# Score, similarity and meta-token matmuls contract 128 partitions, with zero halves per head

## The chip, the core and the metric

The kernel runs on one core of a Trainium2 chip. The metric is the device time of one execution in microseconds (us), the median of several runs. TensorE (PE in the profile) multiplies matrices into PSUM, ScalarE (ACT) and VectorE (DVE) do the work on elements, GpSimd (POOL) is almost unused, and SyncE (SP) issues the loads.

## The reference

A trunk of two layers over 272 tokens (16 learned meta tokens and 256 of the sequence), width 1024. The change touches the two token mixers of a layer:

```python
# retention, per head (64 wide q and k, 128 wide v), both directions, in chunks
s   = einsum(q, k) * decay_in
o   = einsum(s, v) + einsum(q * decay, state)
# attention, 8 query heads on 2 key heads, 64 wide, window of 128 and the meta tokens for all
s_band = where(valid, einsum(qb, kband) * scale, -1e30)
s_meta = einsum(qb, meta_k) * scale
p = softmax(concat([s_sink, s_meta, s_band]))
o = einsum(p_meta, meta_v) + einsum(p_band, vband)
...
```

Both read projections of the normed input (`u @ w_in`) and feed `w_ret_o` and `w_att_o`; then come gates, `w_mix_o`, and a squared-ReLU MLP.

## The kernel before

The whole state lies in SBUF with channels on partitions and the 272 tokens (`T`) along the free dimension. Weights come from HBM in units of 128 x 1024, one after another in the order of use; `unit` rounds each to a high part (`wh`, ACT, L128) and a remainder (`wl`, DVE, L129), in rings of four. Every product is three matmuls of such parts, high x high, high x low, low x high (`mm3`, L133 to L135), so precision is kept at the fast matmul type (fp32r). `product` and `proj` run 8 x 3 of them for one output block of 128 channels.

Attention and retention need single heads, which are 64 wide, so two heads lie on one tile of 128 partitions. The high x high and one mixed product of a head are taken in one matmul of 128 rows, by laying the high part on one half of the partitions and the low part on the other (`ka[0]`, `ka[1]`, `qa`, `qk`). The remaining mixed product is a matmul over the 64 partitions of that head alone: L520 in `score` (with `ka[2]`) and L615 in `similar` (with `ql`).

The 16 meta tokens are handled as groups of 32 columns (2 heads x 16): three groups in 96 columns or partitions (`thrice`, `kblk`, `vblk`, `vm`, `vmp`, `pmk`, `ptm`, `tm`), high, low and high again. `meta` (L585) multiplies the meta keys in `kblk` by the queries in three matmuls (L594).

The order of the work is written out by hand and then fixed by a scheduling layer at build time. `value_r`, `key_a` and `query_a` project the values and attention's keys and queries. Then eight heads of attention run: `score(hh + 1)`, `turned(hh)` (transposes of the softmax), `attended` for each pair of heads; eight heads of retention follow: `similar(hh + 1)`, `retained(hh)`, `normed(hh)`. Between these, `fill(n)` puts matmuls of the remaining projections from `queue` on PE, so that PE has work while ACT and DVE finish a softmax. For layer 0 the meta queries have a softmax of their own (L490 to L506, tiles in `m0`).

Tiles are taken from pools of one, two or four buffers by tag: a new tile of a tag waits until the oldest one of that tag is read for the last time. The tags here are `ex` (the exponentials of softmax), `pn` (the normed probabilities), `ptm`, and for retention `tt` and `tb` (the decay) and `sd` (the decayed similarities).

## Time and profile before

| | |
|---|---|
| median of 3 runs | 910.5 us (909.09 to 910.96) |
| span of the profiled execution, first to last instruction | 907.6 us |
| median less that span (work around the span, and spread) | 2.9 us |
| busy: PE, DVE, ACT, POOL | 893.5, 622.1, 561.0, 0.2 us |
| the chain that ended last, by engine | PE 92%, DVE 4% |

Busy time is the time in which at least one instruction of an engine runs. Matmuls overlap in PE's pipeline, so a row that lasts 0.29 us can be followed by the next one after 0.13 us; what a matmul costs is the distance from its start to the next one's. The profile's own time is that of one execution; the runs are timed by themselves.

### The profile page before, as it was taken

What the parts mean: (1) busy time and instruction counts of PE and PEld (TensorE: products, weight loads), DVE (VectorE), ACT (ScalarE), POOL (GpSimd) and SP (SyncE); (2) the same over time, 40 slices, a digit from 0 to 9 for tenths busy, and PEclk for the clock granted to TensorE, in tenths of its full rate; (3) what the DMA queues carried; (4) which work ended last, traced back from release to release, by engine and by line L of the source; (5) the groups of instructions that cost most, each with busy time, mean ns of one, the idle gap of its engine ahead of it and who ended that gap; (6) DMA issues with size and microseconds to landing.
All of it is one profiled execution on the core that took longest, in us unless ns stands there. A gap on an engine that the chain in (4) does not pass through costs nothing.

```text
span 907.6 us, 16590 instructions
## 1 busy us (share of the span) xinstructions
PE 893.5 (98%) x6506; PEld 846.6 (93%) x6506; DVE 622.1 (69%) x1215; ACT 561.0 (62%) x1038; POOL 0.2 (0%) x4
## 2 busy tenths in 40 slices
PE   9999999999999999999999999999999999999997
PEld 8999998999999999999989989989999999998885
DVE  7898888777668655444459898887777765554443
ACT  6757767666467777543455577776665588783432
POOL 0000000000000000000000000000000000000000
PEclk9999999999999999999999999999999999999999
DMA  7653433345554656555544544433456466666661
GB/s 249 197 158 94 140 117 97 113 147 163 181 163 126 200 165 181 168 183 168 181 118 146 157 121 136 139 117 117 128 160 188 129 198 201 188 205 185 183 189 70
DMA packets 41838, 142.15 MB, mean 157 GB/s; under 512 B 5408, under 2 KB 7584, under 8 KB 41760
## 3 DMA queue, kind: packets, MB, share of 16 engines
q1 hardware_dynamic: 41616, 140.96, 51.2%
q8 instruction: 51, 0.84, 0.4%
q14 instruction: 27, 0.22, 0.1%
q10 hardware_dynamic: 144, 0.13, 0.0%
HBM read 140.02 MB, written 1.05 MB: 155 GB/s over the span
## 4 chain that ended last, share of the span: by engine, by line
PE 92%; DVE 4%; ACT 1%; DMA 1%; SPq 1%; issue 1%; DVEq 0%; ACTq 0%
PE ps_a L133 15%; PE ps_a L134 14%; PE ps_a L135 14%; PE ps_s L135 5%; PE ps_s L134 5%; PE ps_s L133 5%; PE ps_t L133 4%; PE ps_t L134 4%; PE ps_t L135 4%; PE ps_s L781 2%; PE ps_a L781 2%; PE ps_a L780 2%; PE ps_s L780 2%; PE ps_a L782 2%; PE ps_s L782 2%; PE ps_o L554 2%
## 5 line engine op out<-in xcount | busy, mean ns | idle before, releaser
L129 DVE TENSOR_TENSOR wl<-raw,wh 128x1024 fp32r<-128x1024 f32 (+2 forms) x264 | 318.2, 1207 | 209.0 <-ACT wh L128 207.1
L128 ACT ACTIVATE wh<-raw 128x1024 fp32r<-128x1024 f32 (+2 forms) x261 | 272.4, 1045 | 218.9 <-PE ps_a L134 74.3
L133 PE MATMUL ps_a<-uh,wh 128*128 128x272 f32 (+1 forms) x920 | 271.0, 295 | 3.8 <-ACT uh L230 3.1
L135 PE MATMUL ps_a<-uh,wl 128*128 128x272 f32 (+1 forms) x920 | 263.3, 286 | 0.0
L134 PE MATMUL ps_a<-ul,wh 128*128 128x272 f32 (+1 forms) x920 | 263.1, 286 | 0.2
L133 PEld LDWEIGHTS ps_a<-uh,wh 128*128 128x128 f32 x920 | 173.4, 188 | 7.7 <-ACT uh L230 3.7
L134 PEld LDWEIGHTS ps_a<-ul,wh 128*128 128x128 f32 x920 | 173.3, 188 | 2.2 <-DVE ul L88 0.8
L135 PEld LDWEIGHTS ps_a<-uh,wl 128*128 128x128 f32 x920 | 173.2, 188 | 0.6 <-DVE wl L129 0.3
L135 PE MATMUL ps_s<-uh,wl 128*128 128x272 f32 (+1 forms) x184 | 53.4, 290 | 0.3 <-DVE wl L129 0.3
L134 PE MATMUL ps_s<-ul,wh 128*128 128x272 f32 (+1 forms) x184 | 53.1, 288 | 0.0
L133 PE MATMUL ps_s<-uh,wh 128*128 128x272 f32 (+1 forms) x184 | 53.0, 289 | 0.0
L133 PE MATMUL ps_t<-uh,wh 128*128 128x272 f32 (+1 forms) x144 | 41.3, 287 | 1.3 <-ACT uh L230 1.3
L134 PE MATMUL ps_t<-ul,wh 128*128 128x272 f32 (+1 forms) x144 | 41.2, 286 | 0.0
L135 PE MATMUL ps_t<-uh,wl 128*128 128x272 f32 (+1 forms) x144 | 41.1, 285 | 0.0
L135 PEld LDWEIGHTS ps_s<-uh,wl 128*128 128x128 f32 x184 | 35.3, 192 | 0.7 <-DVE wl L129 0.7
L133 PEld LDWEIGHTS ps_s<-uh,wh 128*128 128x128 f32 x184 | 35.4, 192 | 0.0
L134 PEld LDWEIGHTS ps_s<-ul,wh 128*128 128x128 f32 x184 | 35.3, 192 | 0.0
L133 PEld LDWEIGHTS ps_t<-uh,wh 128*128 128x128 f32 x144 | 27.2, 189 | 1.5 <-ACT uh L230 1.5
L92 DVE TENSOR_TENSOR fl<-ft,fh 128x272 fp32r<-128x272 f32 (+1 forms) x64 | 27.6, 433 | 0.9 <-ACT fh L91 0.9
L91 ACT ACTIVATE fh<-ft 128x272 fp32r<-128x272 f32 (+1 forms) x64 | 27.1, 424 | 1.7
L709 ACT ACTIVATE ft<-ft 128x272 f32<-128x272 f32 (+1 forms) x64 | 27.1, 424 | 1.6
L133 PE MATMUL ps_a<-fh,wh 128*128 128x272 f32 x96 | 27.8, 290 | 0.0
(296 smaller groups left out, 1937.8 us busy)
## 6 DMA issues: line engine op xcount, KB each, us to landing
raw<-in_w SPq DMA_DIRECT2D x258, 512.0 KB, 3.6
h<-in_h_in SPq DMA_DIRECT2D x8, 136.0 KB, 2.9
tab<-in_tabs SPq DMA_DIRECT2D x2, 544.0 KB, 5.4
out<-yt SPq DMA_DIRECT2D x3, 256.0 KB, 2.0
raw<-in_w SPq DMA_DIRECT2D x4, 128.0 KB, 3.3
raw<-in_w SPq DMA_DIRECT2D x2, 256.0 KB, 4.5
gj<-in_grow SPq DMA_DIRECT2D x1, 512.0 KB, 4.7
mats<-in_mats SPq DMA_DIRECT2D x1, 320.0 KB, 5.2
```

The lines of the kernel that those rows point to most:

```text
L91: A.activation(xh, x, AF.Copy)
L92: V.tensor_tensor(out=xl, in0=x, in1=f(xh), op=sub)
L128: rounded.append(A.activation(wh[:, c], raw[:, c], AF.Copy).ins)
L129: V.tensor_tensor(out=wl[:, c], in0=raw[:, c], in1=f(wh[:, c]), op=sub)
L133: PE.matmul(ps, ah, bh, start=first, stop=False)
L134: PE.matmul(ps, ah, bl, start=False, stop=False)
L135: return PE.matmul(ps, al, bh, start=False, stop=last)
L554: PE.matmul(po[:, c0:], va_pad[c][:, 64 * gg:64 * gg + P], pts[2 * t + gg][:, c, c0:], start=gg == 0 and c == 0, stop=False)
L709: A.activation(t2[:, c0:], t1[:, c0:], AF.Square)
L780: PE.matmul(pss[i], xh, wh[:, sl], start=kk == 0, stop=False)
L781: PE.matmul(pss[i], xh, wl[:, sl], start=False, stop=False)
L782: PE.matmul(pss[i], xl, wh[:, sl], start=False, stop=kk == KF - 1)
```

## The change

The low parts get tiles of their own, of 128 partitions with zeros in the half of the other head: `kal` for attention's keys, and `ql1` beside `ql` for the odd heads of retention. L520, L615 and the third matmul of `meta` then contract 128 partitions. The meta groups become four of 32 (128 columns or partitions); the fourth is low x low, and `meta` runs a fourth matmul. The remainder groups of `vm` and `vmp` are now two ranges of partitions (`odds`), each with an instruction of its own. The constants that must be zero are cleared by GpSimd. To make room, `ex` uses the buffers of `tt`, `ptm` those of `tb`, and `pn` those of `sd`.

```diff
     def zeros(shape, name, dt=F32):
         t = const.tile(shape, dt, name=name)
-        V.memset(f(t) if dt == F32R else t, 0.0)
+        nc.gpsimd.memset(f(t) if dt == F32R else t, 0.0)
         return t
 
-    kblk = [zeros([P, 4, 3, 32], f"kblk{i}", F32R) for i in range(3)]
-    vblk = zeros([P, 3, 32], "vblk")
-    lows, highs = slice(32, 64), slice(64, 96)
-
-    def thrice(x):
-        return x.unsqueeze(1).to_broadcast([x.shape[0], 3, 16])
+    kblk = [zeros([P, 4, 4, 32], f"kblk{i}", F32R) for i in range(3)]
+    vblk = zeros([P, 4, 32], "vblk")
+    kal = zeros([P, 2, T], "kal", F32R)
+    ql1 = zeros([P, 4, T], "ql1", F32R)
+    lows, odds = slice(64, 128), (slice(32, 64), slice(96, 128))
+
+    def fourfold(x):
+        return x.unsqueeze(1).to_broadcast([x.shape[0], 4, 16])
...
-                    low = vm[highs, 4 * q:4 * q + 4]
-                    V.tensor_tensor(out=low, in0=tpm[highs], in1=f(low), op=sub)
+                    for r in odds:
+                        low = vm[r, 4 * q:4 * q + 4]
+                        V.tensor_tensor(out=low, in0=tpm[r], in1=f(low), op=sub)
...
-            for a in halves:
-                V.tensor_tensor(out=ka[2][a], in0=r[a], in1=f(ka[a is halves[1]][a]), op=sub)
+            for a in range(2):
+                V.tensor_tensor(out=kal[halves[a], a], in0=r[halves[a]], in1=f(ka[a][halves[a]]), op=sub)
...
-        V.tensor_copy(vmp, tp[:96, 256:384])
-        V.tensor_tensor(out=vmp[highs], in0=tp[highs, 256:384], in1=f(vmp[highs]), op=sub)
+        V.tensor_copy(vmp, tp[:, 256:384])
+        for r in odds:
+            V.tensor_tensor(out=vmp[r], in0=tp[r, 256:384], in1=f(vmp[r]), op=sub)
...
+        ql = slot("10b", "ql", (4, T), F32R), ql1
+        nc.gpsimd.memset(f(ql[0][halves[1]]), 0.0)
...
-                        V.tensor_tensor(out=ql[hi, i, cc:], in0=r[hi, cc:], in1=f(x), op=sub)
+                        V.tensor_tensor(out=ql[a][hi, i, cc:], in0=r[hi, cc:], in1=f(x), op=sub)
...
-            ex = two.tile([P, T + 1], F32, tag="ex", name="ex")
+            ex = two.tile([P, T + 1], F32, tag="tt", name="ex")
...
-            for c in range(3):
+            for c in range(4):
...
                 PE.matmul(ps[:, :T], qa[:, gg, t, sl], ka[gg], start=True, stop=False)
-                PE.matmul(ps[:, :T], qa[r, gg, t, sl], ka[2][r], start=False, stop=True)
+                PE.matmul(ps[:, :T], qa[:, gg, t, sl], kal[:, gg], start=False, stop=True)
...
-                pn = two.tile([P, SEQ], F32, tag="pn", name="pn", bufs=4)
+                pn = four.tile([P, SEQ], F32, tag="sd", name="pn")
...
-                ptm = two.tile([96, T], F32R, tag="ptm", name="ptm")
+                ptm = two.tile([P, T], F32R, tag="tb", name="ptm")
...
-            ps = bank("s", [T])[:96]
-            for i, q in enumerate((qk[0][:, 0, t], qk[0][:, 1, t], ql[:, t])):
-                PE.matmul(ps[:, c0:], kblk[i][:, t], q[:, c0:], start=i == 0, stop=i == 2)
...
+            ps = bank("s", [T])
+            for i, q in enumerate((qk[0][:, 0, t], qk[0][:, 1, t], ql[0][:, t], ql[1][:, t])):
+                PE.matmul(ps[:, c0:], kblk[min(i, 2)][:, t], q[:, c0:], start=i == 0, stop=i == 3)
...
                 PE.matmul(ps[:, c0:T], qk[1][:, gg, t, sl], qk[0][:, gg, t, c0:], start=True, stop=False)
-                PE.matmul(ps[:, c0:T], qk[1][r, gg, t, sl], ql[r, t, c0:], start=False, stop=True)
+                PE.matmul(ps[:, c0:T], qk[1][:, gg, t, sl], ql[gg][:, t, c0:], start=False, stop=True)
```

Line numbers of the kernel after are two to four higher in this part of the program. PE's order around the first two steps of retention in layer 0, before (L594 is the meta product, L614 and L615 are a similarity step, L133 to L135 fill):

```order
824 L594 MATMUL ps_s<-qk,kblk_113 96x272
825 L594 MATMUL ps_s<-qk,kblk_115 96x272
826 L594 MATMUL ps_s<-ql,kblk_117 96x272
...
833 L614 MATMUL ps_s<-qk,qkl 128x272
834 L615 MATMUL ps_s<-ql,qkl 128x272
835 L614 MATMUL ps_s<-qk,qkl 128x272
836 L615 MATMUL ps_s<-ql,qkl 128x272
```

The same place on PE after the change (L598, L617 and L618 are those lines now; ql_123 is the tile `ql1`):

```order
824 L598 MATMUL ps_s<-qk,kblk_113 128x272
825 L598 MATMUL ps_s<-qk,kblk_115 128x272
826 L598 MATMUL ps_s<-ql,kblk_117 128x272
827 L598 MATMUL ps_s<-ql_123,kblk_117 128x272
...
834 L617 MATMUL ps_s<-qk,qkl 128x272
835 L618 MATMUL ps_s<-ql_123,qkl 128x272
836 L617 MATMUL ps_s<-qk,qkl 128x272
837 L618 MATMUL ps_s<-ql_123,qkl 128x272
```

The meta product has a fourth matmul, the similarity step for an odd head reads `ql1`, and nothing else has moved here. DVE's order in the value projections of layer 0, where `vm` is written (wl is the rounding of weights, tt the decay for retention), before:

```order
44 L129 TENSOR_TENSOR wl<-raw,wh 128x1024
45 L372 TENSOR_TENSOR vm<-ps_s,vm 32x512
46 L361 COPY pads<-vt 128x3x16
47 L129 TENSOR_TENSOR wl<-raw,wh 128x1024
48 L88 SCALAR_TENSOR_TENSOR tab<-tab,rb 128x272 x2
49 L327 TENSOR_TENSOR t_443<-ps_a,tab 128x272
50 L129 TENSOR_TENSOR wl<-raw,wh 128x1024
51 L328 STREAM_SHUFFLE t_444<-t_443 128x272
52 L608 TENSOR_TENSOR tt<-tt,tb 128x128
```

The same place on DVE after the change:

```order
41 L129 TENSOR_TENSOR wl<-raw,wh 128x1024
42 L375 TENSOR_TENSOR vm<-ps_s,vm 32x512 x2
43 L129 TENSOR_TENSOR wl<-raw,wh 128x1024
44 L329 TENSOR_TENSOR t_447<-ps_a,tab 128x272
45 L88 SCALAR_TENSOR_TENSOR tab<-tab,rb 128x272
46 L330 STREAM_SHUFFLE t_448<-t_447 128x272
47 L129 TENSOR_TENSOR wl<-raw,wh 128x1024
```

The instruction on `vm` is doubled, and the product of `tt` and `tb` has left. ACT's order at the end of attention in layer 0 shows where the decay of retention is built after the change (`pn` belongs to the last score, L609 to L611 are the exponentials for `tt` and `tb`, L594 here is the `tb` of `meta`):

```order
119 L529 ACTIVATE pn<-ex,rs 128x256 x2
120 L609 ACTIVATE tt<-rel,de 128x256
121 L610 ACTIVATE tt<-rel,de 128x144
122 L128 ACTIVATE wh<-raw 128x1024
...
130 L550 ACTIVATE ptm<-ps_t 128x272
131 L611 ACTIVATE tb<-rel,de 128x128
132 L128 ACTIVATE wh<-raw 128x1024
133 L594 ACTIVATE tb<-relm,dem 128x16
```

Before, the first two of these sets stood in the value projections, ahead of attention; now they stand behind the last softmax.

## Rows read from the trace of the kernel before

**Rows 1.** The page: span, and busy time of the engines

```profile
span 907.6 us, 16590 instructions
...
PE 893.5 (98%) x6506; PEld 846.6 (93%) x6506; DVE 622.1 (69%) x1215; ACT 561.0 (62%) x1038; POOL 0.2 (0%) x4
```

**Rows 2.** Waits of PE: total us, times, longest

```profile
PE ps_s L364 <- DVE pads L361: 0.6, 1, 0.6
```

**Rows 3.** PE in time, first similarity step, layer 0: start, duration, instruction, operands

```profile
134.44 0.29 PE L135 MATMUL ps_a<-uh,wl 128*128 128x272 f32 x1
134.57 0.28 PE L614 MATMUL ps_s<-qk,qkl 128*128 128x272 f32 x1
134.78 0.39 PE L615 MATMUL ps_s<-ql,qkl 64*128 64x272 f32 x1
135.10 0.39 PE L614 MATMUL ps_s<-qk,qkl 128*128 128x272 f32 x1
135.42 0.39 PE L615 MATMUL ps_s<-ql,qkl 64*128 64x272 f32 x1
135.74 0.39 PE L133 MATMUL ps_a<-uh,wh 128*128 128x272 f32 x1
135.97 0.29 PE L134 MATMUL ps_a<-ul,wh 128*128 128x272 f32 x1
```

**Rows 4.** PE in time, a later step of retention, layer 0

```profile
151.51 0.42 PE L594 MATMUL ps_s<-qk,kblk 128*96 128x272 f32 x2
151.77 0.29 PE L594 MATMUL ps_s<-ql,kblk 128*96 128x272 f32 x1
151.89 0.29 PE L133 MATMUL ps_a<-uh,wh 128*128 128x272 f32 x1
...
152.90 0.49 PE L133 MATMUL ps_a<-uh,wh 128*128 128x272 f32 x1
153.22 0.29 PE L134 MATMUL ps_a<-ul,wh 128*128 128x272 f32 x1
...
157.72 0.49 PE L626 MATMUL ps_o<-tm,vm 96*128 96x272 f32 x1
158.05 0.29 PE L133 MATMUL ps_a<-uh,wh 128*128 128x272 f32 x1
```

**Rows 5.** Lines L520, L615: count, min/median/max ns, first and last start

```profile
L520 PE MATMUL ps_s<-ka,qa x32: 385/388/393, 62.1 to 576.0; 64*128 64x272 f32 x32
L615 PE MATMUL ps_s<-ql,qkl x32: 378/384/391, 134.8 to 643.5; 64*128 64x272 f32 x16, 64*128 64x256 f32 x16
```

**Rows 6.** Windows: stretch, length, busy per engine (instructions), clock, DMA

```profile
45.00:62.00 17.00, 16.47 (x127) 16.13 (x127) 16.22 (x40) 8.90 (x14) 0.00 (x0) 1.00 0.56 169
91.99:109.05 17.06, 17.06 (x122) 15.63 (x120) 14.34 (x42) 11.47 (x28) 0.00 (x0) 1.00 0.44 125
549.87:566.07 16.20, 16.20 (x119) 14.90 (x118) 14.14 (x43) 12.22 (x30) 0.00 (x0) 1.00 0.39 128
604.00:642.00 38.00, 38.00 (x268) 34.78 (x268) 28.95 (x63) 22.43 (x50) 0.00 (x0) 1.00 0.40 119
```

**Rows 7.** Lines L372 and L608 on DVE: count, min/median/max ns

```profile
L372 DVE TENSOR_TENSOR vm<-ps_s,vm x4: 689/689/689, 31.1 to 514.5; 32x512 fp32r<-32x512 f32 x4
L608 DVE TENSOR_TENSOR tt<-tt,tb x16: 274/284/294, 35.8 to 630.7; 128x128 f32<-128x128 f32 x16
```

**Rows 8.** DVE, ACT, PE in time: first softmaxes of layers 0 and 1

```profile
63.13 0.35 DVE L398 TENSOR_SCALAR m<-t 64x16 f32<-64x16 f32 x2
...
63.53 0.72 PE L492 MATMUL ps_s<-m 128*128 128x272 f32 x2
...
526.17 0.49 ACT L525 ACTIVATE pn<-ex,rs 128x256 f32<-128x256 f32 x1
...
527.04 0.44 PE L532 MATMUL ps_t<-mats,pn 128*128 128x128 f32 x2
```

**Rows 9.** Line L272 on DVE: clearing constants

```profile
L272 DVE MEMSET kblk<- x3: 378/378/378, 1.0 to 1.8; 128x384 f32 x3
L272 DVE MEMSET vblk<- x1: 138/138/138, 2.2 to 2.2; 128x96 f32 x1
```

More of the change, by code (lines that the diff above doesn't have):

```diff
@@ L331, in rotated @@
             return t2
-        pads = slot("10a", "pads", (4, 192))
-        vtm = pads[:, 0:2].rearrange("p a (b c k) -> p (a b) c k", b=2, c=3)
-        va_pad = [pads[:, 2], pads[:, 3]]
+        pads = slot("10a", "pads", (896,))
+        vtm = pads[:, 0:512].rearrange("p (a c k) -> p a c k", a=4, c=4)
+        va_pad = [pads[:, 512:704], pads[:, 704:896]]
         V.memset(pads, 0.0)
         vr = slot(2, "vr", (2, D))
-        vm = one.tile([96, 8, P], F32R, tag="vm", name="vm")
+        vm = one.tile([P, 8, P], F32R, tag="vm", name="vm")
         if l == 0:
@@ L342, in encoder @@
             m0 = slot(7, "m0", (2176,))
-            qblk, pm, pmblk, pmt, ka0 = (m0[:, a:b] for a, b in ((0, 512), (512, 784), (784, 1168), (1168, 1424), (1424, 1696)))
+            qblk, pm, pmblk, pmt, ka0 = (m0[:, a:b] for a, b in ((0, 512), (512, 784), (784, 1296), (1296, 1552), (1552, 1824)))
             V.memset(qblk, 0.0)
         es_sb, mask, rel_sb, relm_sb, skn, skmn, de, dem = cst
-        ka = [one.tile([P, T], F32R, tag=f"ka{i}", name="ka") for i in range(3)]
+        ka = [one.tile([P, T], F32R, tag=f"ka{i}", name="ka") for i in range(2)]
         halves = slice(0, 64), slice(64, 128)
@@ L355, in value_r @@
             if m == 0:
-                tpv[q] = bank("s", [4, P])[:96], [bank("t") for _ in range(2)]
+                tpv[q] = bank("s", [4, P]), [bank("t") for _ in range(2)]
             tpm, tps = tpv[q]
@@ L360, in value_r @@
             mine = vtm[:, m]
-            V.tensor_copy(mine[:, :, 16 * (m % 2):16 * (m % 2) + 16], thrice(vt[:, 0:16]))
+            V.tensor_copy(mine[:, :, 16 * (m % 2):16 * (m % 2) + 16], fourfold(vt[:, 0:16]))
             def centre():
@@ L411, in encoder @@
             stt(tab[:, i], tab[:, i], -0.5, rb)
-        vmp = one.tile([96, P], F32R, tag="vmp", name="vmp")
+        vmp = one.tile([P, P], F32R, tag="vmp", name="vmp")
         for gg in range(2):
-            V.tensor_copy(vblk[64 * gg:64 * gg + 64, :, 16 * gg:16 * gg + 16], thrice(vat[64 * gg:64 * gg + 64, 0:16]))
+            V.tensor_copy(vblk[64 * gg:64 * gg + 64, :, 16 * gg:16 * gg + 16], fourfold(vat[64 * gg:64 * gg + 64, 0:16]))
         tp = bank("t")
@@ L495, in encoder @@
             V.tensor_scalar(out=pm, in0=ex[:, :T], scalar1=rs, scalar2=None, op0=mul)
-            for c in range(3):
+            for c in range(4):
                 V.tensor_tensor(
-                    out=pmblk.rearrange("p (t c g k) -> p t c g k", t=4, c=3, g=2)[:, :, c],
+                    out=pmblk.rearrange("p (t c g k) -> p t c g k", t=4, c=4, g=2)[:, :, c],
                     in0=mat["blk"].rearrange("p (t g k) -> p t g k", t=4, g=2),
@@ L511, in score @@
             t, gg = hh // 2, hh % 2
-            r = slice(64 * gg, 64 * gg + 64)
             if gg == 0:
-                pmk[t] = two.tile([P, 2, 3, 32], F32, tag="pmk", name="pmk")
+                pmk[t] = two.tile([P, 2, 4, 32], F32, tag="pmk", name="pmk")
             pns[hh] = []
@@ L519, in score @@
                 PE.matmul(ps[:, :T], qa[:, gg, t, sl], ka[gg], start=True, stop=False)
-                PE.matmul(ps[:, :T], qa[r, gg, t, sl], ka[2][r], start=False, stop=True)
+                PE.matmul(ps[:, :T], qa[:, gg, t, sl], kal[:, gg], start=False, stop=True)
                 rs = four.tile([P, 1], F32, tag="rs", name="rs")
                 ex = softmax(ps, mask[:, it], skn[:, l, hh:hh + 1], rs)
-                V.tensor_scalar(out=pmk[t][:, it, :, 16 * gg:16 * gg + 16], in0=thrice(ex[:, 0:16]), scalar1=rs, scalar2=None, op0=mul)
-                pn = two.tile([P, SEQ], F32, tag="pn", name="pn", bufs=4)
+                V.tensor_scalar(out=pmk[t][:, it, :, 16 * gg:16 * gg + 16], in0=fourfold(ex[:, 0:16]), scalar1=rs, scalar2=None, op0=mul)
+                pn = four.tile([P, SEQ], F32, tag="sd", name="pn")
                 A.activation(pn, ex[:, 16:T], AF.Copy, scale=rs)
@@ L539, in turned @@
                 t = hh // 2
-                tp = bank("t", [T])[:96]
+                tp = bank("t", [T])
                 for it in range(2):
@@ L543, in turned @@
                 if l == 0:
-                    PE.matmul(tp[:, 0:16], pmblk[:, 96 * t:96 * t + 96], es_sb, start=True, stop=True)
-                ptm = two.tile([96, T], F32R, tag="ptm", name="ptm")
+                    PE.matmul(tp[:, 0:16], pmblk[:, P * t:P * t + P], es_sb, start=True, stop=True)
+                ptm = two.tile([P, T], F32R, tag="tb", name="ptm")
                 A.activation(ptm[:, c0:], tp[:, c0:], AF.Copy)
@@ L625, in retained @@
                 PE.matmul(po[:, c0:], vr[:, c, hh * P:(hh + 1) * P], sds[hh][c][:, c0:], start=c == 0, stop=False)
-            PE.matmul(po[:, c0:], vm[:, hh], tm[:96, t, c0:], start=False, stop=True)
+            PE.matmul(po[:, c0:], vm[:, hh], tm[:, t, c0:], start=False, stop=True)
             pvs[hh] = square(po[:, c0:], c0)
```

12 lines of the change are left out of this document (5 added, 7 removed).

## The prediction

> **What bounds the kernel now.** I read the page's first lines, then PE's waits, then PE's rows one by one. The busy line [rows 1] says PE 893.5 of a span of 907.6 us, so 14.1 us of idle time in all. PE's list of waits for other engines adds little to that; the one entry that this text needs is in [rows 2]. So time goes where PE's queue goes, and a change is worth what it takes out of the spacing of PE's starts, as long as nobody else becomes late. "Busy" can't show that spacing, since matmuls overlap: a plain row reads 0.29 us, yet the next one starts 0.125 us later. The reader should therefore subtract start times.
>
> [Rows 3] is one such stretch, a whole similarity step. L135 to L614 is 0.13 us. Then L614 (128 rows) to L615 (64 rows) is 0.21, L615 to the next L614 0.32, that to L615 0.32, L615 to L133 0.32, and L133 to L134 still 0.23, before the plain 0.125 returns. Every row around a matmul of 64 rows is late, on the way in and on the way out, without any wait for a semaphore. [Rows 4] shows what does not do this: the meta products with 96 columns of weights start 0.13, 0.13 and 0.12 us apart. And a step with 96 rows, L626, takes 0.33 us to its successor, but so does the full L133 at 152.90 (0.32): both are the first fp32r matmul after plain fp32 ones, so this is a price of that change of type and not of 96 rows.
>
> **The change part by part.** *The 64-row matmuls become 128-row ones.* In [rows 3] five matmuls, from 134.57 to 135.97, take 1.40 us; at 0.125 each they would take 0.63, so a step gives back 0.775. L520 and L615 stand there 32 times each [rows 5], two to a step: 32 steps, 24.8 us. Steps that are taken apart (two singles, as at the start of attention) lose the same by halves. I take off 0.4 us for first matmuls that follow fp32 and stay late: **24.4 us**. The lower bound is that only the way out of the 64-row matmul, 0.32 for 0.125, is gained: 64 times 0.195, 12.5 us.
>
> On this the Trainium skill speaks against the change. Its page "TensorE: Matmul & The Clock Gate", Part 3 (Packing small matmuls), says that the weight load of a matmul overlaps a running one only where the two use different row groups, and advises to cut small contractions into row groups so that they run beside each other. By that rule 64-row matmuls would be no dearer than full ones and zero padding would bring nothing: 0 in place of 24.4 us. The rows here show plain 128-row matmuls 0.125 us apart and 64-row ones 0.32.
>
> *A fourth meta group.* L594 runs three matmuls for each of 4 values of t in each of 2 layers; a fourth, at 0.125, costs **1.0 us**. 96 columns or rows becoming 128 cost PE nothing by [rows 4]. The copies that widen from 48 to 64 elements lie on DVE and are hundredths of a microsecond each.
>
> So PE's own queue shrinks by 24.4 - 1.0 = **23.4 us**. What of this arrives depends on DVE.
>
> *DVE gets work in a stretch where it is full.* The rounding remainder of vm is now two instructions in place of one: L372, 0.69 us, four times [rows 7], becomes eight; two of the four extra ones lie before attention in each layer. In layer 0 DVE is busy 16.22 of 17 us there [rows 6], and PE already waits for it once (L364 for pads, 0.6 us, [rows 2]). In exchange two L608 of 0.28 us [rows 7] leave this stretch, since their tile now shares buffers with ex and must follow attention. Net +0.8 us of DVE. The place where it shows is L492: its fourth matmul starts at 63.53, and the DVE instruction that feeds it, L398, ends at 63.48 [rows 8]. There is no slack; DVE comes 0.8 later and PE 0.4 sooner (one single 64-row matmul lies ahead of it, half of 0.775), so PE waits 1.2 us. Behind L492 on PE are the products that fill the time, and the softmaxes of the first heads wait on the same DVE queue, so most of those two heads' gain waits too: I take 0.8 more, **2.0 us** in layer 0 (bounds 0.5 and 3.5). In layer 1 the first transpose (L532) starts at 527.04 and its input, pn, ends at 526.17 + 0.49 = 526.66 [rows 8]: 0.38 us of slack, and PE comes some 1.1 us sooner (one step, 0.775, and a single), while DVE is later by one small instruction: **1.0 us** (0 to 2).
>
> *Attention proper.* A period of two heads takes 17.06 us in layer 0 and 16.20 in layer 1, with DVE busy 14.34 and 14.14 [rows 6]. PE would now need 17.06 - 1.55 = 15.5 and 14.65. DVE still fits, but at 93 and 97%, and softmax makes it alternate with ACT. The rings of weights and the order of scores ahead of transposes let DVE fall some microseconds behind without PE noticing. I take **1.0 us** for the two layers (0 to 11, see the second rival).
>
> *Covered edits.* The exps and products that similarity builds its decay from move behind the last softmax; ACT has room (11.47 of 17.06 us [rows 6]), and 18 plain matmuls of PE's queue still stand between the last attended step and the first similarity step. If they came late, the first sd of each layer would be late by their 1 to 2 us. Retention keeps DVE at 28.95 of 38 us [rows 6], so its gain of 0.775 a step is safe. Shared buffers of pn and sd, ptm and tb are free by then in program order. The cleared constants move to GpSimd; nothing reads them before 62 us (L520's first start, [rows 5]) except DVE's own writes. Taking them off DVE I cost at nothing too: they stand ahead of the first ul, which also needs h, gains and uh; what they could bring is bounded by their 1.3 us (three of 378 ns and one of 138, [rows 9]).
>
> Sum: -24.4 + 1.0 + 2.0 + 1.0 + 1.0 = -19.4. The profiled execution has a span of 907.6; the median of the runs is 910.5, 2.9 more, which I take as the part around the span. 907.6 - 19.4 = 888.2, plus 2.9 is **891 us**.
>
> **The rivals.** *All of PE's gain arrives*: the weights' rings and the filling products hide DVE's extra 0.8 us and the short slack. For it: PE hardly waits now. Against: the two places in [rows 8] have no slack. 910.5 - 23.4 = 887.
>
> *DVE becomes the bound in attention*: if the softmax chain needs the idle time that DVE now has (2.1 us in 16.2), a period of two heads can't get shorter at all, and the 16 score steps give nothing: 23.4 - 12.4 = 11.0, less little, 900. For it: 97% in layer 1. Against: that idle time holds waits for ACT's wh, which themselves wait for PE to free a buffer, so they shrink with PE's period.
>
> *The gap isn't made by the row count* but by something that stays, such as the operands being split at partition 64: then only the fourth group and DVE's work are felt, about +1 to +2 us, 912. It is what the rule of the Trainium skill's page above would lead to. Against: L614 and L615 differ in nothing else that the rows show.
>
> *GpSimd's clears come late, and the kernel is slower.* The trace has no long memset on GpSimd; its four of one column take 0.2 us together [rows 1]. DVE needs 378 ns for 384 columns [rows 9], 1 ns a column. kal is the fifth to be cleared, after 2208 columns counting itself, and DVE's write into it holds DVE's queue. The low part is first used at 62.1 us. To lose 25 us (the gain and 1.8, 0.2% of the time) the clear would have to end near 87 us, 39 ns a column. A rate at which it ends before DVE's first write to kal is free. Nothing in the trace speaks for such a rate, nothing excludes it.
>
> **How the numbers follow.** Forecast (most of PE's gain, less 2 to 7 us of waits for DVE) 0.58; all of it 0.25; DVE the bound 0.12; gap stays 0.03; GpSimd late 0.02. The time is the forecast's, 891. The range, 886 to 898, takes in the first rival with a microsecond of spread between runs, and most of the way to the second; outside lie about 1.5 in 10. Under 0.2% (1.8 us) a measurement of this kernel can't tell from no change, as the three runs spread by that much. Faster: 0.58 + 0.25 + 0.12 = 0.95; the third rival is on the border, 0.02 same and 0.01 slower, and with GpSimd slower is 0.03.
>
> **What would show it.** In the profile after, the rows that answer to [rows 3] start 0.125 us apart right through L615's successor, and PE's busy time is about 870. Four rows of the meta product stand 0.125 apart. PE's waits list DVE (pads, the m0 tile, ex's chain through pn) with 2 to 4 us at the start of each attention stage. If the starts are plain but the span falls by less than 15, DVE's busy share in attention should be near 100% and PE's waits there many. If the second matmul of each pair still starts 0.2 to 0.3 late, the step on row counts is wrong. If kal's clear on POOL ends after DVE's first write to kal could have started, that clear was mis-sized.

## The result, and the profile after

The changed kernel takes **896.6 us** (median of four runs, 895.27 to 897.48) against 910.5 before; the ratio is 0.9844, with a 95% interval of 0.9831 to 0.9857. The forecast was 891, with a range of 886 to 898. The sign and the cause are as forecast, and the time lies in the range, but 5.6 us of the forecast gain of 19.4 did not arrive. The profiled execution took 895.3 us; it is the fastest of the four.

The page after, span and busy times, to be read against [rows 1]:

```profile
span 893.5 us, 16615 instructions
...
PE 874.2 (98%) x6514; PEld 841.2 (94%) x6514; DVE 620.5 (69%) x1218; ACT 560.9 (63%) x1038; POOL 5.2 (1%) x12
```

PE's busy time fell by 19.3 us, the span by 14.1. The chain that ended last shows the same from its side: PE's share is now 77% of it, DVE's 12% and ACT's 7%.

First the gain. PE in time after the change, the first similarity step of layer 0, which answers to [rows 3] (L617 is the full product, L618 the former 64-row one):

```profile
130.77 0.29 PE L135 MATMUL ps_a<-uh,wl 128*128 128x272 f32 x1
130.89 0.29 PE L617 MATMUL ps_s<-qk,qkl 128*128 128x272 f32 x1
131.02 0.29 PE L618 MATMUL ps_s<-ql,qkl 128*128 128x272 f32 x1
131.15 0.29 PE L617 MATMUL ps_s<-qk,qkl 128*128 128x272 f32 x1
131.27 0.29 PE L618 MATMUL ps_s<-ql,qkl 128*128 128x272 f32 x1
131.40 0.29 PE L133 MATMUL ps_a<-uh,wh 128*128 128x272 f32 x1
131.52 0.29 PE L134 MATMUL ps_a<-ul,wh 128*128 128x272 f32 x1
```

Every start is 0.12 to 0.13 us behind the one before. From the first L617 to L134 it is 0.63 us where [rows 3] had 1.40: 0.77 for a step, as the prediction worked out. The meta product has its fourth matmul at the plain distance too; here is a later one of layer 0 (x2 means two instructions merged in the row), where four take 0.51 us:

```profile
146.86 0.42 PE L598 MATMUL ps_s<-qk,kblk 128*128 128x272 f32 x2
147.11 0.41 PE L598 MATMUL ps_s<-ql,kblk 128*128 128x272 f32 x2
147.37 0.29 PE L133 MATMUL ps_a<-uh,wh 128*128 128x272 f32 x1
```

Now the loss. The waits of PE for other engines after the change, total, times and longest:

```profile
PE ps_a L133 <- ACT uh L230: 2.8, 2, 1.4
PE ps_t L536 <- ACT pn L529: 1.9, 3, 0.9
...
PE ps_s L497 <- DVE m L401: 1.0, 1, 1.0
PE ps_s L617 <- DVE tmx L88: 0.7, 1, 0.7
PE ps_s L366 <- DVE pads L363: 0.5, 1, 0.5
```

The first entry is old (3.1 us before). The others are the transposes of the softmax (L536), the scores of the meta queries (L497), a similarity step (L617) and the centre product (L366); of these only the last was in the list of before [rows 2]. They don't add up to all that is missing, since a fill product that PE runs early during a wait is no gain either. So I set the starts of the same matmul in both traces against each other. The table is worked out from the starts of L133, the first matmul of a weight tile's product, at the borders named; "gained" is by how much the changed kernel's lead over the one before grew between them.

| stretch of the program | gained, us | if PE alone decided |
|---|---|---|
| layer 0 up to the third score step | 0.1 | 2.3 |
| layer 0, five more score steps and the first similarity step | 4.2 | 4.7 |
| layer 0, second similarity step and first meta product | -0.5 | 0.7 |
| layer 0, the other six similarity steps | 4.3 | 4.3 |
| layer 1, value projections | -1.2 | 0 |
| layer 1, from there to the second score step | 0.0 | 1.6 |
| layer 1, score steps 3, 4, 6 and 8 | 2.9 | 3.1 |
| layer 1, score steps 5 and 7 (transposes of heads 3 and 5) | -0.1 | 1.6 |
| layer 1, first two similarity steps and first meta product | 0.2 | 1.4 |
| layer 1, the other six similarity steps | 4.3 | 4.3 |

The second column has 0.775 for each step that lies between the borders, less 0.125 for a meta product. Of its 23.8 us, 14.2 arrived. In the steady stretches of attention a step gains 0.69 to 0.74 us; nearly all that is lost is lost at six places, where DVE or ACT is late.

Ahead of attention in layer 0 such a lead says little, since two executions of one and the same kernel differ there. In a second trace of the changed kernel (e10 below) PE is 1.3 us further behind from 17 us on. Its granted clock between 10 and 20 us was 0.66, where the first trace has 0.83 (1.00 is 2.4 GHz, 0.5 is 1.2 GHz), with PE busy for 9.8 of the 10 us in both. From the first softmax on, the gains of the two traces agree within 0.2 us at every place of the table.

Layer 0's attention in the window that [rows 6] show, with the same columns:

```profile
91.99:109.05 17.06, 17.06 (x134) 16.75 (x133) 16.12 (x46) 13.18 (x32) 0.00 (x0) 1.00 0.49 144
```

DVE is busy 94% of it, where it was 84%, and PE still does not wait: 134 matmuls lie in the window where there were 122. That is layer 0; what happens at two places of layer 1 is told with e6 and e12.

GpSimd in time, the cleared constants:

```profile
0.74 1.45 POOL L272 MEMSET kblk<- 128x512 f32 x3 [0.29 <-POOLq L909]
2.12 0.20 POOL L272 MEMSET vblk<- 128x128 f32 x1
2.27 0.56 POOL L272 MEMSET kal<- 128x544 f32 x1
2.76 1.01 POOL L272 MEMSET ql<- 128x1088 f32 x1
3.83 1.00 POOL L432 MEMSET ql<- 64x1088 f32 x1
```

For the large ones that is 0.9 to 1.0 ns a column, and all of them are over at 4.8 us. One more clear of `ql`, for layer 1, runs at 455.7 us, and no instruction waits for it. That rival is out.

### The profile page after: what moved, and what is told of

Read it like the earlier page. It is cut to its first block, busy times and chain, and to the rows that moved or that the text cites. A ratio compares the mean times of both kernels' runs of the same rounds, so it can differ in the third digit from the quotient of the medians.

```text
span 893.5 us, 16615 instructions
## 1 busy us (share of the span) xinstructions
PE 874.2 (98%) x6514; PEld 841.2 (94%) x6514; DVE 620.5 (69%) x1218; ACT 560.9 (63%) x1038; POOL 5.2 (1%) x12
## 3 DMA queue, kind: packets, MB, share of 16 engines
HBM read 140.02 MB, written 1.05 MB: 158 GB/s over the span
## 4 chain that ended last, share of the span: by engine, by line
PE 77%; DVE 12%; ACT 7%; issue 2%; DMA 1%; SPq 1%; DVEq 0%; ACTq 0%
PE ps_a L133 11%; PE ps_a L134 11%; PE ps_a L135 11%; PE ps_s L133 5%; PE ps_s L135 5%; PE ps_s L134 5%; PE ps_t L133 4%; PE ps_t L134 4%; PE ps_t L135 4%; DVE wl L129 3%; ACT wh L128 2%; PE ps_s L784 2%; PE ps_a L784 2%; PE ps_a L783 2%; PE ps_a L785 2%; PE ps_s L783 2%
## 5 line engine op out<-in xcount | busy, mean ns | idle before, releaser
L129 DVE TENSOR_TENSOR wl<-raw,wh 128x1024 fp32r<-128x1024 f32 (+2 forms) x264 | 318.3, 1207 | 210.5 <-ACT wh L128 208.8
L133 PE MATMUL ps_a<-uh,wh 128*128 128x272 f32 (+1 forms) x920 | 269.4, 293 | 3.4 <-ACT uh L230 2.8
L134 PE MATMUL ps_a<-ul,wh 128*128 128x272 f32 (+1 forms) x920 | 263.6, 287 | 0.4
L135 PE MATMUL ps_a<-uh,wl 128*128 128x272 f32 (+1 forms) x920 | 263.5, 287 | 0.2 <-DVE wl L129 0.2
L133 PEld LDWEIGHTS ps_a<-uh,wh 128*128 128x128 f32 x920 | 173.5, 189 | 5.8 <-ACT uh L230 3.2
L134 PEld LDWEIGHTS ps_a<-ul,wh 128*128 128x128 f32 x920 | 173.2, 188 | 2.3 <-DVE ul L88 1.3
L135 PEld LDWEIGHTS ps_a<-uh,wl 128*128 128x128 f32 x920 | 173.3, 188 | 1.0 <-DVE wl L129 0.8
L135 PE MATMUL ps_s<-uh,wl 128*128 128x272 f32 (+1 forms) x184 | 53.2, 289 | 0.3 <-DVE wl L129 0.3
L133 PE MATMUL ps_s<-uh,wh 128*128 128x272 f32 (+1 forms) x184 | 53.0, 289 | 0.1
L134 PE MATMUL ps_s<-ul,wh 128*128 128x272 f32 (+1 forms) x184 | 53.0, 288 | 0.0
L133 PE MATMUL ps_t<-uh,wh 128*128 128x272 f32 (+1 forms) x144 | 41.3, 287 | 1.3 <-ACT uh L230 1.3
L134 PE MATMUL ps_t<-ul,wh 128*128 128x272 f32 (+1 forms) x144 | 41.3, 287 | 0.0
L135 PE MATMUL ps_t<-uh,wl 128*128 128x272 f32 (+1 forms) x144 | 41.1, 285 | 0.0
L135 PEld LDWEIGHTS ps_s<-uh,wl 128*128 128x128 f32 x184 | 35.2, 191 | 0.7 <-DVE wl L129 0.7
L133 PEld LDWEIGHTS ps_s<-uh,wh 128*128 128x128 f32 x184 | 35.2, 191 | 0.5 <-ACT wh L128 0.5
L134 PEld LDWEIGHTS ps_s<-ul,wh 128*128 128x128 f32 x184 | 35.2, 191 | 0.0
L133 PEld LDWEIGHTS ps_t<-uh,wh 128*128 128x128 f32 x144 | 27.2, 189 | 1.5 <-ACT uh L230 1.5
L133 PE MATMUL ps_s<-fh,wh 128*128 128x272 f32 x96 | 27.8, 290 | 0.0
```

What stands on the lines that cost most here:

```text
L129: V.tensor_tensor(out=wl[:, c], in0=raw[:, c], in1=f(wh[:, c]), op=sub)
L133: PE.matmul(ps, ah, bh, start=first, stop=False)
L134: PE.matmul(ps, ah, bl, start=False, stop=False)
L135: return PE.matmul(ps, al, bh, start=False, stop=last)
```

## The experiments

The four theories behind the first runs: the row count is the whole gain (mine), DVE binds attention so that score steps bring nothing, the gap is made by something else, and what is lost is the price of the fourth meta group and of shared buffers, as against an order that the scheduler happened to choose.

**e4_rows64: the changed kernel without its core.** All side edits stay (four groups, two `vm` remainders, shared buffers, clears on GpSimd); the 64-row products come back, and with them three meta matmuls.

```diff
-                PE.matmul(ps[:, :T], qa[:, gg, t, sl], kal[:, gg], start=False, stop=True)
+                PE.matmul(ps[:, :T], qa[64 * gg:64 * gg + 64, gg, t, sl], ka[2][64 * gg:64 * gg + 64], start=False, stop=True)
...
-                PE.matmul(ps[:, c0:T], qk[1][:, gg, t, sl], ql[gg][:, t, c0:], start=False, stop=True)
+                PE.matmul(ps[:, c0:T], qk[1][64 * gg:64 * gg + 64, gg, t, sl], ql[64 * gg:64 * gg + 64, t, c0:], start=False, stop=True)
```

> The changed kernel without its core: the low parts of score and similarity stay in 64-row matmuls (ka2 and one ql for both heads, three meta matmuls), while the four meta groups, the doubled instructions on vm and vmp, the shared buffers and the clears on GpSimd are as in the change. My theory: no gain on PE is left, and the price of the rest shows: 911 to 914. Rival (the gain comes from the groups of 128 rows or from the order of work, not from the 64-row matmuls): 897 to 905.

Measured: 912.42 us, ratio 1.0018 (1.0005 to 1.0031). The side edits cost 2 us and gain nothing; the row count brings the 15.8 us from here to the changed kernel. By the starts of L133, 1.6 us are lost in layer 1's value projections and 0.9 in layer 0's first three score steps; ahead of those this execution is 0.7 us in front of the one of the kernel before, with a granted clock of 1.00 between 10 and 15 us against 0.70.

**e1_kal: the kernel before with the score step alone padded.**

```diff
+    kal = zeros([P, 2, T], "kal", F32R)
...
-                PE.matmul(ps[:, :T], qa[r, gg, t, sl], ka[2][r], start=False, stop=True)
+                PE.matmul(ps[:, :T], qa[:, gg, t, sl], kal[:, gg], start=False, stop=True)
```

> The kernel before, with one part of the change: attention's low key parts get the zero-padded tile kal, so that the second matmul of every score step contracts 128 rows. Similarity keeps its 64 rows, the meta groups stay three, the buffers stay apart. My theory (each step with 64-row matmuls loses 0.775 us on PE): 16 score steps give 12.4 us on PE, less the waits seen in the attention stages of the changed kernel (some 1.7 us in layer 0 and 3 in layer 1), so 902 to 904 us, and the score rows of the profile start 0.125 us apart. Rival (the spacing isn't made by the row count): 910, with the second matmul of a pair still 0.2 us late. Rival (DVE is the bound in attention): 907 or more, with plain spacing but as much lost in waits.

Measured: 899.25 us, ratio 0.9877 (0.9846 to 0.9908). Sixteen steps gave 11.4 us by the medians (8.4 to 14.0 by the interval) of the 12.4 that [rows 3] promise, and 10.0 by the starts of L133 from the first softmax on. In layer 1 each score step from the third on gained 0.58 to 0.78, those at heads 3 and 5 too. What is missing is missing at the start of attention: 0.9 us in layer 0's first three steps and 1.0 in layer 1's first two. So DVE does not bind attention, and behind its start it keeps up with PE's faster pace as long as it has only the old work. I had expected 902 to 904 and was too careful by 3 us.

**e5_adjacent: is it the 64-row matmul or the switch to it?** In the kernel before, both full products of a similarity step come first, then both 64-row ones. Row counts stay.

```diff
                 PE.matmul(ps[:, c0:T], qk[1][:, gg, t, sl], qk[0][:, gg, t, c0:], start=True, stop=False)
+                both.append((ps, sl))
+            for c in range(2):
+                ps, sl = both[c]
                 PE.matmul(ps[:, c0:T], qk[1][r, gg, t, sl], ql[r, t, c0:], start=False, stop=True)
```

> The kernel before; only the order within a similarity step is another: both 128-row matmuls first, then both 64-row ones (full, full, 64, 64 in place of full, 64, full, 64). Row counts stay. If the cost sits in the switch between row counts, two 64-row matmuls stand 0.125 us apart and one switch in and one out fall away: the five rows take about 1.01 in place of 1.40 us, 0.39 for each of 16 steps, -6.2 us: 904 to 905 (before 910.6). If each 64-row matmul is dear by itself (0.32 us to whatever follows), the two stay 0.32 apart and a step saves 0.195, -3.1 us: 907 to 908. If adjacency changes nothing: 910.6.

Measured: 904.11 us, ratio 0.9927 (0.9912 to 0.9941). Each of the 16 steps gained 0.36 to 0.42 us by the starts of L133 (0.39 in the switch theory, 0.195 in the other). PE in time in this run, the first similarity step of layer 0 (L618 is its 64-row product), which answers to [rows 3]:

```profile
136.16 0.41 PE L614 MATMUL ps_s<-qk,qkl 128*128 128x272 f32 x2
136.51 0.39 PE L618 MATMUL ps_s<-ql,qkl 64*128 64x272 f32 x1
136.74 0.28 PE L618 MATMUL ps_s<-ql,qkl 64*128 64x272 f32 x1
136.95 0.39 PE L133 MATMUL ps_a<-uh,wh 128*128 128x272 f32 x1
137.19 0.29 PE L134 MATMUL ps_a<-ul,wh 128*128 128x272 f32 x1
137.31 0.29 PE L135 MATMUL ps_a<-uh,wl 128*128 128x272 f32 x1
```

From the first L614 to the first L618 it is 0.35 us, 0.13 to the second L614 and 0.22 from there. Then come 0.23 to the second L618, 0.21 to L133 and 0.24 to L134, before the plain 0.125 returns: 1.03 us from the first L614 to L134, where [rows 3] have 1.40. The total is that of the switch theory, but its picture is not: two 64-row matmuls side by side don't stand 0.125 us apart. What fits is that each change of row count costs 0.09 us on the row that changes and 0.1 on the row behind it, the same into the 64 rows as out of them. In [rows 3] the three rows at 0.32 are such a change right behind another and pay both, 0.125 + 0.09 + 0.1. Four changes make the 0.775 us of a step there, and two make the 0.39 that is left here. The price is that of the change from one row count to the other. The Trainium skill's page "TensorEngine Tiling (Array Packing)", section Key Properties, says that a change of the tiling mode, not of the tile alone, drains TensorE; it gives no price. The rows agree that the change of row count costs time, and put one at 0.19 us. That it is a drain, and that a change of the tile alone costs nothing, no run here shows.

This run also shows a loss of 1.6 us ahead of attention that its edit can't explain, since the edit lies behind it: its layer 0 projections wait 2.0 us for `pads`, where [rows 2] have 0.6. PE came to that place 1.4 us sooner, with a granted clock of 1.00 between 10 and 15 us (0.70 in the kernel before), while DVE wrote `pads` at the same time as before. Between 45 and 50 us, where the wait lies, the granted clock was 0.66, and 1.00 in the kernel before.

**e2_three: the changed kernel with three meta groups.** One `vm` and one `vmp` remainder, 96 columns and partitions; the fourth group, low x low, is left out, as before the change. The meta product keeps its four matmuls, since the low parts of the queries lie in two tiles.

```diff
-    lows, odds = slice(64, 128), (slice(32, 64), slice(96, 128))
+    lows, odds = slice(32, 64), (slice(64, 96),)
...
-        return x.unsqueeze(1).to_broadcast([x.shape[0], 4, 16])
+        return x.unsqueeze(1).to_broadcast([x.shape[0], 3, 16])
```

> The changed kernel with three meta groups of 32, as before (96 rows or columns), so that the remainder of vm and vmp is one DVE instruction again; the zero-padded kal and ql1, the fourth meta matmul, the shared buffers and the clears on GpSimd stay. My theory (part of what the forecast missed is the extra 0.69 us of DVE, four times, where DVE is full): about 2 us faster than the changed kernel, 894 to 895.5, with the 1.2 us that layer 1 lost in the value projections back. Rival (DVE's load in general, which hardly changes here, is what holds PE): within 0.7 us of the changed kernel, 896 to 897. Rival (96 rows cost PE something that 128 do not): slower than the changed kernel, 899 or more.

Measured: 891.29 us, ratio 0.9782 (0.9759 to 0.9805): 5.3 us better than the changed kernel by medians, 3.9 by the spans (889.6 and 893.5). The fourth group costs 2 to 2.6 times what I gave it. By the starts of L133, 1.3 us of it come in layer 0's first three score steps, and in layer 1 1.0 in the value projections, 0.6 at the first two heads, 1.0 at head 3 and 0.6 at head 5; ahead of attention in layer 0 this execution is 0.7 us behind the one of the changed kernel. Not all of the loss at the start of attention goes with the fourth group: with three groups 0.9 us are still missing in layer 0's first three steps and 1.0 in layer 1's first two, as in e1.

**e3_three_ex: e2 with buffers of its own for ex.**

```diff
-            ex = two.tile([P, T + 1], F32, tag="tt", name="ex")
+            ex = two.tile([P, T + 1], F32, tag="ex", name="ex")
```

> As the run with three meta groups, and the exponentials of softmax (ex) have buffers of their own again, so that the decay of retention (tt) need not wait for the last softmax; pn and sd, ptm and tb still share. My theory (sharing makes retention start late, some 1.1 us in each layer): 1.5 to 2.5 us faster than with three groups alone, 892 to 893.5, and the waits around the first similarity and meta steps are gone. Rival (the late start of retention comes from DVE's queue, not from the buffers): no faster than with three groups alone.

Measured: 889.79 us, ratio 0.9766 (0.9739 to 0.9793), span 887.9. It is 1.5 us faster than e2 by medians and 1.7 by spans; the two intervals overlap, so the traces have to say where. The start of layer 0's retention takes 1.0 us less, so there it is the decay behind the last softmax that was late. The start of layer 1's takes 0.5 us more, with a wait for `tmx` of 1.2 us in place of 0.8: the waits that I expected to go are gone in layer 0 alone. The rest of the 1.7 us comes ahead of that, and in large part from the clock. The window from 10 to 15 us, with the columns of [rows 6], in e2 and then in e3:

```profile
10.00:15.00 5.00, 4.58 (x20) 3.72 (x19) 3.29 (x8) 3.89 (x8) 0.00 (x0) 0.70 0.94 331
10.00:15.00 5.00, 4.65 (x28) 3.73 (x28) 2.99 (x7) 3.59 (x8) 0.00 (x0) 1.00 0.98 351
```

In this window e3 gets 1.4 us ahead, before anything that its edit touches. So buffers of its own for `ex` are worth 1.0 us in layer 0, and the runs don't show that they are worth more. This is the fastest of the kernels here, 6.8 us ahead of the changed one by medians.

What stands on ACT there is seen in the changed kernel. ACT in time at the end of layer 0's attention, ahead of the similarity step shown above:

```profile
129.90 0.41 ACT L611 ACTIVATE tb<-rel,de 128x128 f32<-128x128 f16 x1 [1.79 <-DVE tmx L595]
```

The exponential into `tb` waits 1.79 us for DVE to read the `tb` ahead of it (L595, which ran at 129.70 behind two weight remainders), and holds what stands behind it on ACT. This wait alone is not what was new: the same place waits 1.3 us in e3, and a like one in the kernel before does too.

**e7_before_shared: the kernel before with the shared buffers alone** (`ex` with `tt`, `pn` with `sd`, `ptm` with `tb`: the three lines of the change's diff that name these tags).

> The kernel before with the shared buffers alone (ex with the decay's tt, pn with sd, ptm with tb); 64 rows and three groups stay. If sharing costs by itself, by holding the decay's exps behind the last softmax: +1.5 to +3 us, 912 to 913.5, with PE waiting at the start of retention. If it costs only once PE is faster (the old pace hides it): 910.6 within a microsecond.

Measured: 909.23 us, ratio 0.999 (0.998 to 0.9999). Sharing costs nothing at the old pace. It is PE's faster pace that uncovers it.

**e6_three_spare: e2 with the second vm remainder as idle work.**

```diff
                         V.tensor_tensor(out=low, in0=tpm[r], in1=f(low), op=sub)
+                        V.tensor_tensor(out=spare[r], in0=tpm[r], in1=f(low), op=sub)
```

> e2_three (three meta groups, 891.3) with one idle DVE instruction more after each of the four vm remainders, of the same form (32x512, from the same PSUM bank, into a buffer that nobody reads). If the doubled vm instruction is what the fourth group costs: 895 to 896.6, with the waits of the centre product for pads and of the m0 scores back. If what the fourth group costs lies elsewhere (wider copies, the fourth matmul, where the scheduler puts things): 891 to 892.5.

Measured: 893.25 us, ratio 0.9806 (0.9785 to 0.9827), span 890.8. That is 2.0 us above e2 by medians, 1.2 by spans, between my two cases. In its trace the wait for `m` is 1.0 us again, as in the changed kernel (0.4 in e2), and layer 0's first three score steps gain 0.6 us less than in e2. PE also waits 2.5 us for `pads` in layer 0, but the changed kernel has no such wait there (its 0.5 us lies in layer 1), and it isn't the added instruction's: ahead of it ACT waits for a weight, and DVE stands idle for ACT.

```profile
38.95 1.06 ACT L128 ACTIVATE wh<-raw 128x1024 fp32r<-128x1024 f32 x1 [2.94 <-DMA raw<-in_w]
40.44 0.43 DVE L389 TENSOR_TENSOR kal<-t,ka 64x272 fp32r<-64x272 f32 x1 [2.60 <-ACT ka L387]
```

In layer 1 e6 loses 0.3 us more than e2 at the first two heads, and at no other place. So the instruction's time explains about half of the 1.3 us that the fourth group costs in layer 0, and not the places in layer 1. The order on DVE there differs between e6 and the changed kernel. DVE in time in the changed kernel, at head 3 of layer 1 (L489 is the masked minimum of a softmax, L129 the remainder of a weight tile):

```profile
536.44 1.22 DVE L129 TENSOR_TENSOR wl<-raw,wh 128x1024 fp32r<-128x1024 f32 x1
537.57 0.42 DVE L331 TENSOR_TENSOR t<-ps_a,tab 128x256 f32<-128x256 f32 x1
537.91 0.50 DVE L489 CUSTOM_DVE_ANT_0 ps_s<-ps_s,mask,skn 128x272 f32<-128x272 f32 x1
```

The same place in e6_three_spare (lines two higher):

```profile
535.38 0.42 DVE L331 TENSOR_TENSOR t<-ps_a,tab 128x256 f32<-128x256 f32 x1
535.73 0.50 DVE L491 CUSTOM_DVE_ANT_0 ps_s<-ps_s,mask,skn 128x272 f32<-128x272 f32 x1
...
536.90 1.22 DVE L129 TENSOR_TENSOR wl<-raw,wh 128x1024 fp32r<-128x1024 f32 x1
```

In the changed kernel the scheduler put one remainder of 1.22 us ahead of head 3's softmax, in e6 behind it. In layer 1's value projections it did the like: the pair of `vm` remainders stands ahead of the copy into `pads` for which PE's centre product waits, in e6 behind it. The changed kernel there, DVE and PE:

```profile
485.24 1.39 DVE L375 TENSOR_TENSOR vm<-ps_s,vm 32x512 fp32r<-32x512 f32 x2 [0.63 <-ACT vm L372]
486.67 0.20 DVE L363 COPY pads<-vt 128x64 f32<-128x64 f32 x1
...
486.92 0.49 PE L366 MATMUL ps_s<-mats,pads 128*128 128x128 f32 x2 [0.53 <-DVE pads L363]
```

**e9_one_edge, e10_after_again and e12_own_softmax: that one remainder behind the softmax.** The changed kernel with one edge of order, and the changed kernel again beside e9. `mins` lists the softmax minima as they are issued, and 152 is the weight tile in question. In e9 the edge leads to the last minimum issued, which is head 4's; in e12 to head 3's second, as in e6.

```diff
-            V.tensor_tensor(out=wl[:, c], in0=raw[:, c], in1=f(wh[:, c]), op=sub)
+            with tc.issue_after(mins[EDGES[i]]) if i in EDGES else nullcontext():
+                V.tensor_tensor(out=wl[:, c], in0=raw[:, c], in1=f(wh[:, c]), op=sub)
```

> The changed kernel with a single edge of order added: the rounding remainder (wl) of one weight tile of layer 1's attention is held behind the softmax of head 3, as the scheduler has it in e6_three_spare; the rest of layer 1's order on DVE then follows e6's. Nothing is computed otherwise. If what e6 leaves unexplained of the fourth group's cost (after 896.6, e6 893.3) is the place that the scheduler gave this remainder: 894.0 to 895.2, with the two waits of layer 1's transposes for pn (0.9 and 0.7 us) gone. If it is the fourth group's own work (wider copies, four more matmuls): 896 to 897.

> The changed kernel once more, beside e9 on the same chip: 895.5 to 897.5, as measured first.

> The changed kernel with the same single remainder held behind head 3's own second softmax minimum (in e9_one_edge it was held behind head 4's, which had been issued before it). DVE's sequence of remainders and softmaxes in layer 1's attention is then that of e6_three_spare; layer 0 stays as in the changed kernel. If the place of this remainder costs what the traces show at heads 3 to 5 of layer 1 (0.9 + 0.6 us, and little given back): 894.3 to 895.5 beside 896.4 for the changed kernel. If the time is lost again at the next head, as in e9: 896 to 899.

Measured: e9 899.30 us, ratio 0.9884 (0.9866 to 0.9901); the changed kernel again 896.26, ratio 0.9849 (0.9827 to 0.9871); e12 893.83, ratio 0.9819 (0.9803 to 0.9834). e9 fell outside both its cases. Its trace shows where: head 3 did gain the 1.0 us, and then 3.0 were lost, where the scheduler took two remainders past head 4's softmax. DVE and PE in e9, where the remainders start 4.6 us after the second of their `wh` was there (542.18 plus 1.05 on ACT):

```profile
547.84 2.36 DVE L131 TENSOR_TENSOR wl<-raw,wh 128x1024 fp32r<-128x1024 f32 x2
547.91 0.36 PE L135 MATMUL ps_a<-uh,wh 128*128 128x272 f32 x1 [1.96 <-ACT pn L532]
549.11 0.19 PEld L137 LDWEIGHTS ps_a<-uh,wl 128*128 128x128 f32 x1 [0.94 <-DVE wl L131]
```

The second wait is for a remainder. The first, and larger, is put down to ACT's `pn`; that the moved remainders cause it too is likely from the order, but not shown.

e12 keeps the gain of 0.95 us at head 3 and 0.46 at head 5, and nothing else moves: 1.4 us against the first trace of the changed kernel (spans 892.1 and 893.5), 2.8 and 2.4 by the two medians of that kernel, whose intervals overlap that of e12 at the edge. So one instruction's place on DVE, with what the scheduler then moves behind it, is worth from -1.4 us (by places) to +3 us (by medians) at this pace.

**e11_three_ex_ordered: every remainder behind the last softmax minimum.** In e3_three_ex, the same edge for all weight tiles from the first softmax on, always to the last minimum issued.

> e3_three_ex (889.8) with every weight remainder held behind the last softmax minimum that was issued before it in the program. If remainders ahead of softmaxes are a general loss: 888 to 889.5. If the scheduler's running ahead with the weights is what keeps PE fed: slower than e3, 890.5 to 893, with PE waiting for wl.

Measured: 928.06 us, ratio 1.0203 (1.0180 to 1.0227), 38 us above e3. The sign is that of the second case, and the size more than ten times what I gave it. PE's waits in it begin with

```profile
PE ps_a L137 <- DVE wl L131: 15.2, 13, 2.7
```

In e3 the waits for `wl` are 0.9 us. Part of the 38 us is the clock: it was granted at 0.99 over the whole span, 0.999 in e3, some 8 us by my estimate from the two. That the scheduler runs ahead with the weights, past softmaxes, is what keeps PE fed: the few remainders that it puts in a bad place are the price of a good rule.

**e8_three_ex_fill4: more fill at the start of retention.** e3 with `F[4]`, the matmul groups between the first meta step and the second similarity step, at 4 in place of 2.

> e3_three_ex (889.8) with four in place of two filling products between the first meta step and the second similarity step. If the 1.2 us that PE waits at the start of layer 1's retention is for DVE's meta product alone, two products of 8 x 3 matmuls cover it: 888.5 to 889.3. If the fill is only missing later: 889.5 to 890.5.

Measured: 889.91 us, ratio 0.9770 (0.9756 to 0.9785), the same as e3. The wait of L617 for `tmx` fell from 1.2 to 0.5 us, and the span by 0.6 us, but the runs show nothing of it: it is the second case.

## Why the prediction was right, point by point

*The 64-row matmuls, -24.4.* Right in mechanism and about right in size. The rows stand at 0.125 us, e4 shows that nothing else in the change gains, and e5 that it is the switch of row counts that cost. The lower bound took the way out of the 64 rows to be the dear one; by e5 a change costs 0.19 us in either direction. In steady stretches of attention a step gained 0.72 rather than 0.775. The rule of the Trainium skill's page "TensorE: Matmul & The Clock Gate", Part 3 (Packing small matmuls), which spoke against the change, does not hold here: L617 and L618 use the same rows, and still start 0.125 us apart, so the weight load of one is hidden behind the other. The same Part also lets a load into the background weight buffer run ahead, and the rows fit that.

*The fourth meta matmul, +1.0.* 0.51 us for four, 0.125 each, as costed.

*DVE in layer 0, +2.0.* Measured 2.2 by the third score step. The place was the one named. The cause was DVE's new work for 1.3 us of it; the other 0.9 is missing in e1 and e2 as well, where DVE has one remainder of `vm` as before, and so goes with PE's pace and not with new work. DVE in time in the changed kernel, and the wait of L497:

```profile
63.52 0.28 DVE L427 TENSOR_TENSOR vmp<-ps_t,vmp 32x128 fp32r<-32x128 f32 x1
63.82 0.35 DVE L401 TENSOR_SCALAR m<-t 64x16 f32<-64x16 f32 x2
...
64.22 0.73 PE L497 MATMUL ps_s<-m 128*128 128x272 f32 x2 [0.99 <-DVE m L401]
```

L401 starts at 63.82 where L398 of [rows 8] started at 63.13, 0.7 us later (forecast 0.8), and PE waits 1.0 us (forecast 1.2).

*Layer 1's start, +1.0.* The wait for `pn` at the first transpose was foreseen and is there:

```profile
519.66 0.51 ACT L529 ACTIVATE pn<-ex,rs 128x256 f32<-128x256 f32 x1
...
520.22 0.44 PE L536 MATMUL ps_t<-mats,pn 128*128 128x128 f32 x2 [0.88 <-ACT pn L529]
```

1.6 us of gain are missing at the first two heads; 1.0 of it is missing in e1 and e2 too, and is what the forecast named. But 1.2 more are missing in the value projections ahead of them. This part is **a step that was left out**: the doubled `vm` remainder was costed in layer 1 by its length alone, "DVE is later by one small instruction", and not by what it would stand in front of. e4, at the old pace, loses 1.6 us in this very place.

*Attention proper, +1.0 for both layers.* DVE did go to 94% without PE waiting, as worked out; layer 0 lost 0.5 us. Layer 1 lost 1.7 at heads 3 and 5, of which e12 gave back 1.4 by moving one remainder. The size was wrong, and the cause wasn't DVE's share but its order. The prediction had a sign for this case: plain starts and a span that falls by less than 15 us should mean a DVE near 100% and many waits of PE in attention. The span fell by 14.1, but DVE stood at 94% in layer 0, and PE's waits in attention were few; the sign left no room for losses by order.

*Covered edits, 0.* **This step failed.** The decay's exponentials behind the last softmax were said to be covered, and to cost 1 to 2 us a layer if not. The starts of retention lost 1.2 us in layer 0 and 1.2 in layer 1. e3 gave 1.0 us of it back in layer 0 by unsharing `ex`; e7 shows that at the old pace the cover holds. In layer 1 e3 gave nothing back, so what is lost there stays open. I had counted the matmuls of PE that stand in between, and not the remainders ahead of it on DVE's queue nor the wait for `tb`. The clears on GpSimd and the memsets taken from DVE did cost nothing.

Summed by the table, 9.6 of 23.8 us did not arrive, where 4.4 were forecast (the 4.0 of the three terms and the 0.4 taken off): 2.2 in layer 0's first steps, 1.2 in layer 1's value projections, 1.6 at its first two score steps, 1.7 at heads 3 and 5, 2.4 at the starts of retention, and 0.5 over all the other steps.

*The rivals.* That DVE is the bound in attention fell with e1 (score steps alone: -11.4 us). That the gap is not made by the row count fell with the rows after and with e4. GpSimd's clears end at 4.8 us, but for one that nobody waits for. That all of PE's gain arrives is nearly what e3 shows: without the fourth group and with own buffers for `ex`, 20.9 us arrive by medians (19.7 by spans) of PE's own 23.8.

What stays open: e2 and the changed kernel differ by 5.3 us in the medians and by 3.9 in the spans of the profiled executions, e12 and the changed kernel by 2.4 to 2.8 and 1.4. The runs of one kernel spread by 1 to 3 us, in part with the granted clock of the first 20 us, so how much of the fourth group's cost is DVE's added work and how much the order that came with it is told by places, and not to the last microsecond. That the order is the cause in layer 1's value projections is argued from the rows; only head 3's remainder was moved by itself. Four groups with buffers of its own for `ex` were not run.

## What to carry to other kernels

Where PE is the bound, subtract the starts of its rows and look for changes of shape: a lone matmul over half the rows between full ones cost 0.39 us more than a full one. Zeros in the other half take all of it back on PE, and two such matmuls side by side share one pair of changes and take back half. A gain on PE's queue uncovers every wait that had a few tenths of slack, so list for each place where PE meets DVE or ACT what stands ahead of the awaited instruction on that engine, and how long it is, not only the engine's share. And when a scheduler fixes the order, an edit's side effect on the order (here 1 us gained at one place and up to 3 us lost at another) is of the size of the edit's own small costs; compare the orders before explaining a difference of that size. Look at the granted clock of the first microseconds as well, since it moved one and the same kernel by 1.3 us.

## What the runs showed of the hardware that was not expected

A change between 128 and 64 rows costs 0.19 us in either direction, 0.09 on the row that changes and 0.1 on the row behind it; the second of two 64-row matmuls starts 0.23 us behind the first, as the second full one behind them does (e5). A meta product over 96 columns of weights and one over 128 start at the same distances (0.13 and 0.13 us). GpSimd clears 1088 columns of 4 bytes in 1.0 us for 64 as for 128 partitions; DVE took 378 ns for 384 columns [rows 9], so the two are about alike at this. Between 10 and 15 us the granted clock was 0.59 to 0.70 in some executions and 1.00 in others, with PE busy 4.2 to 4.9 of the 5 us in either case; where it was 1.00, PE was 1.1 to 1.4 us ahead of the execution of the kernel before, which had 0.70, by 16 us.
